# Shorter backlogs for far-ahead transfers, conversions counted in full, and a lighter start, in a conditioned hybrid trunk on eight cores

## The chip, the cores and the metric

The kernel runs on the 8 cores of one Trainium2 chip. Each core handles one batch element with its own copy of the same program; no core talks to another. The metric is the device time of the slowest core, in microseconds (us). In some executions the cores of one die, or of both, show a lower granted TensorE clock and the time is longer, as in one run of the changed kernel: 5797.3 us, with 0.815 on cores 0 to 3 and 0.992 or 0.993 on the others. Such runs are marked and left out. Below, "fast run" means a run without that mark; the fast runs of one kernel in one set lie within 0.3% of each other, except in E7 (0.9%) and E12 (0.6%).

## The reference

Two layers, each with a SwiGLU half step, a mixer and a second SwiGLU half step; shift, scale and gate of every step come from c. Cut to its skeleton:

```python
for l in range(DEPTH):
    mod = silu(c) @ ada_w[l] + ada_b[l]                    # 9 x 1024 values
    y = modulate(rmsnorm(h, norm_g[l, 0]), sh1, sc1)
    h = h + 0.5 * g1 * swiglu(y, ffn1_wg[l], ffn1_wu[l], ffn1_wd[l])
    y = modulate(rmsnorm(h, norm_g[l, 1]), sh2, sc2)
    u, v, q, k, w = split(y @ w_in[l])
    h = h + g2 * (concat(spatial_gating(u, v), dilated_mixture(rope(q), rope(k), w)) @ w_out[l])
    y = modulate(rmsnorm(h, norm_g[l, 2]), sh3, sc3)
    h = h + 0.5 * g3 * swiglu(y, ffn2_wg[l], ffn2_wu[l], ffn2_wd[l])
return rmsnorm(h, final_g)
```

A core has 4096 positions in 8 tiles of 512. The weights arrive as float32 and are turned to bfloat16 once, by transfers from HBM to HBM that convert ("conversions", `wguS<-wgu`, `wdS<-wd`).

## The kernel before

The kernel is a list of thousands of tasks with their dependencies. A scheduler in the program walks through them with a small model of the five engines and of the DMA pipe and writes one fixed instruction order for each engine, with the semaphore waits. On the chip nothing of the model is left but this order. The parts that matter:

```python
def schedule(self, bw=300.0, dlat=2300.0, dmargin=3000.0, cmargin=250.0, backlog=9000.0):
    ...
                if t.dma:
                    if pipe[0] - now > backlog:            # modelled work already in the DMA pipe, ns
                        nxt = min(nxt, pipe[0] - backlog)
                        continue
    ...
            if t.dma:
                pipe[0] = max(pipe[0], st + dur) + t.nbytes / bw
                t.end = pipe[0] + dlat
```

`t.L` is the time by which a task should be done, `hp` the position of the TensorE stream. The start loads c, four constants, tile 0 of x, 16 rows of ada_w (512 KB each), tile 1 of x:

```python
            src = bass.AP(cv.tensor, cv.offset, [[0, 128], [1, D]])          # one row of c to 128 partitions
            G.dma("sp", lambda e: e.dma_start(out=cb, in_=src), 524288, writes=[bcb], name="cb", ...)
    ...
                G.dma("pool", ..., in_=wgu_d[l, w, j]), 1048576, name="guf", ...
                      extra=[first[(10, 12, 14, 15, 19)[min(j, 4)]]] if j < 6 else ())   # first: 16 ada rows, then x tile 1
    ...
            G.chain(ins, [bk], "nsum", pos=pos)            # norm sum of a tile, on TensorE
```

The softmax here doesn't subtract the row's maximum and nothing guards it: scores larger than these inputs give would overflow.

Of the kernel before, what the change touches and what calls it, by code (L numbers as in the profile page):

```python
# [10 lines left out]
ALU = mybir.AluOpType  # L11
# [57 lines left out]
class Graph:  # L69
# [145 lines left out]
    def schedule(self, bw=300.0, dlat=2300.0, dmargin=3000.0, cmargin=250.0, backlog=9000.0):  # L215
# [65 lines left out]
        def pick(e, now):  # L281
# [26 lines left out]
            for t in av:  # L308
# [16 lines left out]
                if t.dma:  # L325
                    if pipe[0] - now > backlog:
                        nxt = min(nxt, pipe[0] - backlog)
                        continue
                    if pipe[0] - now > 3000.0 and any(x.dma and x.eng is None and x.L < t.L and not x.new
                                                      for x in avail["pool" if e == "sp" else "sp"]):  # L330
                        nxt = min(nxt, now + 200.0)
                        continue
# [244 lines left out]
def build_nc():  # L577
# [8 lines left out]
    ada_b = din("ada_b", [128, DEPTH * 72])  # L586
    ngv = din("ngv", [128, DEPTH * 3 * KC])
    fgv = din("fgv", [128, KC])
# [5 lines left out]
    lngb_d = din("lngb", [128, DEPTH * 8])  # L594
# [20 lines left out]
    with ExitStack() as st:  # L615
# [86 lines left out]
        adab = const([128, DEPTH * 72], F32)  # L702
        Av = const([128, DEPTH * 3 * KC], F32)
        Gv = const([128, DEPTH * 3 * KC], F32)
        ng_sb = const([128, DEPTH * 3 * KC], F32)
        fg_sb = const([128, KC], F32)
# [3 lines left out]
        lngb = const([128, DEPTH * 8], F32)  # L710
# [3 lines left out]
        bC = {n: Buf(n) for n in ("ones", "mean", "eps", "ng", "fg", "adab", "lngb", "bc", "ws", "mk")}  # L714
# [18 lines left out]
        sq_more = []  # L733
# [23 lines left out]
        def cond(chunks, pos, slots, cslot, due=None):  # L757
# [4 lines left out]
            tb, btb = tile(slots[0], [128, D], F32, 1, "ct")  # L762
            src = bass.AP(cv.tensor, cv.offset, [[0, 128], [1, D]])
            G.dma("sp", lambda e: e.dma_start(out=cb, in_=src), 524288, writes=[bcb], name="cb", pos=p0,
                  due=None if due is None else due - 150000.0)
            G.op([act(lambda e: e.activation(out=tb, in_=cb, func=AF.Tanh, scale=0.5), 960, "tanh")],
                 reads=[bcb], writes=[btb], name="ctanh", pos=p0)
            G.op([dve(lambda e: e.scalar_tensor_tensor(out=cb, in0=tb, scalar=1.0, in1=cb, op0=ALU.add, op1=ALU.mult), 1150)],
                 reads=[btb], writes=[bcb], name="csilu", pos=p0)
            ring = Ring(slots[1:] + slots[:1], [128, D], F32, "ada")  # L770
            rows = []
            for n, ch in enumerate(chunks):
# [10 lines left out]
                if k in (15, 23):  # L783
# [4 lines left out]
                         reads=[bRow[l][i][part], bC["adab"]], writes=[bm], name="adab", pos=p)  # L788
                    if part == 0:
                        G.op([dve(lambda e, b0=b0, c0=c0: e.scalar_tensor_tensor(  # L790
                            out=Av[:, b0:b0 + KC], in0=modv[:, c0 + 8:c0 + 16], scalar=1.0, in1=ng_sb[:, b0:b0 + KC],
                            op0=ALU.add, op1=ALU.mult), 130)], reads=[bm, bC["ng"]], accw=[bm], name="adaA", pos=p)
# [11 lines left out]
        def load_gu(l, w, j, pos):  # L804
# [3 lines left out]
            if (l, w) == (0, 0) and (l, w, j) not in kept:  # L808
                G.dma("pool", lambda e: e.dma_start(out=ap, in_=wgu_d[l, w, j]), 1048576, writes=[b], name="guf", pos=pos,
                      due={0: -41000.0, 1: -31000.0, 2: -25000.0, 3: -24000.0, 4: -1000.0}.get(j), extra=[first[(10, 12, 14, 15, 19)[min(j, 4)]]] if j < 6 else ())  # L810
# [20 lines left out]
        def conv(l, w, spans, gates=True):  # L831
# [4 lines left out]
            for (j, m), x in zip(items, wt):  # L836
# [8 lines left out]
                if j is not None:  # L845
                    G.dma("pool", lambda e, j=j: e.dma_start(out=wguS[l, w, j], in_=wgu_d[l, w, j]), 1048576,
                          writes=[bWG[l, w, j]], name="cvg", pos=p, extra=[gate])
                else:
                    G.dma("pool", lambda e, m=m: e.dma_start(out=wdS[l, w, m], in_=wd_d[l, w, m]), 1441792,
# [24 lines left out]
        def norm_sum(ht, pos, alts=0):  # L874
# [28 lines left out]
            G.chain(ins, [bk], "nsum", pos=pos)  # L903
# [26 lines left out]
        def norm_out(ht, t, pos, fine=False):  # L930
            rs, brs = norm_sum(ht, pos, 2 if fine else 0)
            for kc in range(KC):
# [4 lines left out]
                     reads=[brs, bC["fg"]], writes=[bh], name="fin", pos=pos)  # L937
# [83 lines left out]
        class Mixer:  # L1021
# [48 lines left out]
            def spatial_tables(self):  # L1070
# [15 lines left out]
                for hd in range(4):  # L1086
# [3 lines left out]
                        reads=[bk, bC["lngb"]], writes=[bC["bc"]], name="bc")  # L1090

            def proj(self, t):
# [104 lines left out]
                def gating(hd, pos):  # L1197
# [9 lines left out]
                        reads=[bk, bC["bc"], bC["lngb"]], writes=[bzt], name="zt", pos=pos)  # L1207
# [244 lines left out]
        for ap, src, n in ((ng_sb, ngv, "ng"), (adab, ada_b, "adab"), (fg_sb, fgv, "fg"), (lngb, lngb_d, "lngb")):  # L1452
            G.dma("sp", lambda e, ap=ap, src=src: e.dma_start(out=ap, in_=src), 65536, writes=[bC[n]], name="const", pos=-20000.0, due=-100000.0)
# [6 lines left out]
        for l in range(DEPTH):  # L1460
# [16 lines left out]
            if l == 0:  # L1477
                for b_ in range(2):
                    for pc_ in range(2):
                        G.dma("pool", lambda e, b_=b_, pc_=pc_: e.dma_start(  # L1480
                            out=mk_sb[:, :, b_ * 256 + pc_ * 128:b_ * 256 + pc_ * 128 + 128],
                            in_=mk_d[:, :, pc_ * 256 + b_ * 128:pc_ * 256 + b_ * 128 + 128]), 196608, accw=[bC["mk"]], name="mk", pos=100000.0,
                              extra=[marks[8][1]])
                conv(0, 0, [(p1 + 40000.0, pg)], False)
                cond(range(16, 48), (p1 + 30000.0, pg - 20000.0), steps(WD0 + 4096, 4096, 3), WD0)
# [128 lines left out]
def _consts():  # L1614
# [11 lines left out]
    for i, (o, k) in enumerate(((pi, n16), (q4, 4 * n16), (n16, n16))):  # L1626
        prev = (k[:, None] >= o[None, :]).astype(np.float32)
        cur = (k[:, None] <= o[None, :]).astype(np.float32)
        masks[:, i] = np.concatenate([prev, prev, cur, cur], 1)
# [19 lines left out]
def _prep_inputs(x, c, ada_w, ada_b, norm_g, ffn1_wg, ffn1_wu, ffn1_wd, ffn2_wg, ffn2_wu, ffn2_wd,  # L1649
# [15 lines left out]
        "ada_b": np.ascontiguousarray(ada_b.reshape(DEPTH, 72, 128).transpose(2, 0, 1).reshape(128, DEPTH * 72)),  # L1665
        "ngv": np.ascontiguousarray(norm_g.reshape(DEPTH, 3, KC, 128).transpose(3, 0, 1, 2).reshape(128, DEPTH * 3 * KC)),
        "fgv": np.ascontiguousarray(f(final_g).reshape(KC, 128).T),
# [4 lines left out]
        "lngb": np.ascontiguousarray(np.concatenate([lng, lnb], 2).reshape(128, DEPTH * 8)),  # L1672
# [19 lines left out]
```

## Time and profile before

| | kernel before |
|---|---|
| fast runs at first | 4884.7 and 4891.1 us |
| spans of the cores | 4860.4 to 4888.1 us |
| TensorE busy, slowest core | 4755.4 us, 97% |
| DMA transfers, share of the chain of waits that ended last | 5% |

TensorE is the bound; what can be won is its idle time, and this lies at the start, around the two mixers and at the end. The lines are in the prediction below. This is SyncE's queue on core 1 where the attention of the first mixer is about to begin (start us, time to hand the transfer over in us, transfer; L1340 below is the first matmul on K):

```profile
684.41 4.87 SPq L825 DMA_DIRECT2D arena<-wdS  x1
689.37 0.51 SPq L1182 DMA_DIRECT2D kS<-arena  x1
689.97 0.97 SPq L1194 DMA_DIRECT2D vS<-arena  x1
691.03 1.26 SPq L1182 DMA_DIRECT2D kS<-arena  x1
...
707.01 0.33 SPq L1271 DMA_DIRECT2D arena<-kS  x1
```

The wdS load at 684.41 us brings down-projection weights, and the next matmul on any such weights comes at 879.45 us. SyncE needs 4.87 us to hand it over (0.33 us for the one at 678.43); that the queue was full is my guess, which no line shows. Only then come the last stores of K. In the chain of waits the K store then takes 15.76 us and the load of K 12.09 us, and TensorE stands still for it (start us, length; idle and what ended it in brackets):

```profile
691.03 15.76 DMA kS<-arena
707.01 12.09 DMA arena<-kS
```

### The profile page before, as it was taken

Reading aid. Unit: us, or ns where it says so; the run is one execution under the profiler, and the core shown is the slowest. Engines: PE = TensorE matmul, PEld = TensorE weight load, DVE = VectorE, ACT = ScalarE, POOL = GpSimd, SP = SyncE. Lnnn points to the kernel's source line nnn. Section 1 sums busy time; section 2 is a strip of 40 time slices with the busy share of each in tenths; the row PEclk is TensorE's granted clock in tenths of the full one; section 3 lists DMA queues with packets and bytes.
Section 4 is the critical chain, followed back from the end, with each engine's and each line's share of the span. In section 5 each row is a group of like instructions: output and inputs, shape, how many; then the busy total and the mean of one; then the engine's idle time right before and its main releaser. Section 6 shows DMA issues by size and latency. Waiting matters only on the chain.

```text
span 4888.1 us, 74266 instructions; the slowest of 8 cores (4860.4 to 4888.1 us)
## 1 busy us (share of the span) xinstructions
PE 4755.4 (97%) x25855; PEld 2250.5 (46%) x25855; DVE 2466.9 (50%) x4087; ACT 2026.2 (41%) x3009; POOL 987.9 (20%) x954
## 2 busy tenths in 40 slices
PE   5999989999999999999999999999999999999998
PEld 2444435454445454444444444454444455544443
DVE  6551556483665473665334326555536554535533
ACT  4111566462755342521311127655537543525311
POOL 0001451112531111300100016312135100122101
PEclk9999999999999999999999999999999999999999
DMA  9987676688475677764721375766665644473414
GB/s 237 200 170 188 169 197 167 180 229 212 157 219 161 186 207 224 213 190 141 243 80 39 92 223 151 209 152 183 154 181 170 193 135 150 118 246 128 142 42 157
DMA packets 376095, 835.32 MB, mean 171 GB/s; under 512 B 151440, under 2 KB 184592, under 8 KB 369296
## 3 DMA queue, kind: packets, MB, share of 16 engines
q1 hardware_dynamic: 356944, 742.08, 49.5%
q0 software_dynamic: 18784, 88.49, 11.8%
q8 instruction: 213, 3.49, 0.3%
q14 instruction: 154, 1.26, 0.1%
HBM read 741.72 MB, written 234.88 MB: 200 GB/s over the span
## 4 chain that ended last, share of the span: by engine, by line
PE 86%; DMA 5%; ACT 3%; DVE 2%; issue 2%; SPq 1%; POOL 1%; DVEq 0%; ACTq 0%; POOLq 0%
PE ps L967 47%; PE ps L995 24%; PE ps L1106 5%; PE ps L1432 4%; PE ps L1374 3%; PE ps L1340 2%; DMA arena<-xP 1%; DMA hS<-arena 1%; DMA arena<-hS 1%; DVE arena L1171 1%; ACT arena L1149 1%; DMA kS<-arena 0%; POOL arena L1147 0%; SPq L778 0%; POOL arena L1178 0%
## 5 line engine op out<-in xcount | busy, mean ns | idle before, releaser
L967 PE MATMUL ps<-arena 128*128 128x512 bf16 x11264 | 2502.9, 380 | 36.2 <-DVE arena L924 28.3
L967 PEld LDWEIGHTS ps<-arena 128*128 128x128 bf16 x11264 | 1082.6, 98 | 1311.9 <-issue 61.2
L995 PE MATMUL ps<-arena 128*128 128x512 bf16 x5632 | 1229.6, 379 | 4.1 <-DVE arena L999 4.1
L973 ACT ACTIVATE arena<-ps 128x512 f32<-128x512 f32 x704 | 418.1, 597 | 1281.3 <-PE ps L967 1277.0
L975 DVE SCALAR_TENSOR_TENSOR arena<-arena,ps 128x512 f32<-128x512 f32 x704 | 480.1, 684 | 765.3 <-ACT arena L973 764.5
L995 PEld LDWEIGHTS ps<-arena 128*128 128x128 bf16 x5632 | 547.1, 98 | 658.2 <-issue 7.5
L999 DVE SCALAR_TENSOR_TENSOR arena<-ps,arena 128x512 f32<-128x512 f32 x256 | 192.0, 750 | 910.1 <-PE ps L995 879.2
L898 POOL TENSOR_TENSOR arena<-arena 128x512 f32<-128x512 f32 (+2 forms) x351 | 414.3, 1180 | 1160.4 <-ACT arena L891 1056.9
L980 DVE TENSOR_TENSOR arena<-ps,arena 128x512 bf16<-128x512 f32 x704 | 483.7, 690 | 211.2 <-PE ps L967 191.3
L1106 PE MATMUL ps<-arena 128*128 128x512 bf16 x2560 | 567.7, 380 | 15.1 <-ACT arena L1190 4.5
L891 ACT ACTIVATE arena<-arena 128x512 bf16<-128x512 f32 x424 | 250.5, 625 | 723.9 <-DVE arena L999 384.6
L1358 ACT ACTIVATE arena<-ps 128x1024 bf16<-128x1024 f32 (+1 forms) x384 | 345.0, 950 | 270.0 <-PE ps L1340 269.1
L1106 PEld LDWEIGHTS ps<-arena 128*128 128x128 bf16 x2560 | 248.7, 98 | 314.3 <-issue 25.2
L1361 DVE TENSOR_TENSOR arena<-arena 128x1024 bf16<-128x1024 bf16 (+1 forms) x384 | 261.5, 687 | 148.7 <-ACT arena L1358 146.4
L926 ACT ACTIVATE arena<-arena 128x512 bf16<-128x512 f32 x372 | 279.5, 806 | 52.3 <-DVE arena L920 51.9
L920 DVE TENSOR_TENSOR arena<-arena 128x512 f32<-128x512 f32 x384 | 271.9, 757 | 35.7 <-ACT arena L906 30.4
L1410 POOL TENSOR_TENSOR arena<-arena 64x512 bf16<-64x512 f32 x128 | 168.4, 1316 | 598.5 <-ACT arena L1405 557.9
L1432 PE MATMUL ps<-arena 128*128 128x512 bf16 x1024 | 225.1, 379 | 2.8 <-DMA arena<-mS 1.8
L1390 DVE TENSOR_TENSOR arena<-ps,arena 128x512 f32<-128x512 f32 x256 | 175.4, 685 | 68.7 <-PE ps L1374 63.1
L1374 PEld LDWEIGHTS ps<-arena 128*128 128x128 bf16 x2736 | 175.4, 98 | 73.8 <-issue 12.9
L1374 PE MATMUL ps<-arena 128*128 128x128 bf16 x2736 | 199.2, 219 | 7.4 <-DVE arena L1361 6.8
L1178 POOL TENSOR_TENSOR arena<-arena 128x512 bf16<-128x512 f32 x128 | 168.4, 1324 | 165.8 <-DVE arena L1169 115.1
(68 smaller groups left out, 2116.0 us busy)
## 6 DMA issues: line engine op xcount, KB each, us to landing
arena<-wguS SPq DMA_DIRECT2D x242, 512.0 KB, 5.6
arena<-hS SPq DMA_DIRECT2D x180, 512.0 KB, 7.9
arena<-wdS SPq DMA_DIRECT2D x128, 704.0 KB, 5.8
arena<-ada_w SPq DMA_DIRECT2D x144, 512.0 KB, 20.1
hS<-arena SPq DMA_DIRECT2D x224, 256.0 KB, 6.2
arena<-hS SPq DMA_DIRECT2D x136, 256.0 KB, 7.8
wguS<-wgu POOLq DMA_DIRECT2D x66, 512.0 KB, 7.8
hS<-arena SPq DMA_DIRECT2D x64, 512.0 KB, 8.2
```

Of the source, the lines that this page charges most:

```text
L898: f = lambda e, a=a, sq=sq, out=out: e.tensor_tensor(out=out, in0=a, in1=sq, op=ALU.add)
L920: f = lambda e, hk=hk, u=u: e.tensor_tensor(out=u, in0=hk, in1=rs, op=ALU.mult)
L926: ga = act(lambda e, hk=hk, A=A, sh=sh, o=o: e.activation(out=o, in_=hk, func=AF.Identity, scale=A, bias=sh), 725)
L967: mate = main([(lambda e, kc=kc, half=half, bk=bk, y=y, gu=gu: e.matmul(bank(bk), lhsT=gu[:, half, kc, :], rhs=y[:, kc, :], start=(kc == 0 ...
L973: G.op([act(lambda e, sg=sg, gb=gb: e.activation(out=smv[sg.i], in_=bank(gb), func=AF.Tanh, scale=0.5), 490, "tanh")], reads=[gb], writes= ...
L975: G.op([dve(lambda e, sg=sg, gb=gb: e.scalar_tensor_tensor(out=smv[sg.i], in0=smv[sg.i], scalar=1.0, in1=bank(gb), op0=ALU.add, op1=ALU.mu ...
L980: G.op([dve(lambda e, sg=sg, ub=ub, o=o: e.tensor_tensor(out=o, in0=bank(ub), in1=smv[sg.i], op=ALU.mult), 610)], reads=[ub, sg], writes=[ ...
L995: main([(lambda e, j=j: e.matmul(bank(bk), lhsT=wd[:, j, :], rhs=a[:, j, :], start=(j == 0), stop=(j == FC - 1)), [bwd, ba[j]], MM) for j ...
L1106: ins.append((lambda e, lhs=lhs, rhs=rhs, kc=kc: e.matmul(bank(bk), lhsT=lhs, rhs=rhs, start=(kc == 0), stop=(kc == KC - 1)), rd + [by[kc] ...
L1358: return e.activation(out=cut(pT, 0), in_=cut(ps[:, :, :], sb.i * 512), func=AF.Exp, scale=0.125)
L1374: return e.matmul(o, lhsT=v[:, vi, h * 64:h * 64 + 128], rhs=pT[:, h, b, pc, :], start=(pc == 0 or not prev), stop=(pc == 1))
L1432: main([(lambda e, kc=kc, m=m, bk=bk: e.matmul(bank(bk), lhsT=w[:, m, kc, :], rhs=mx[:, kc, :], start=(kc == 0), stop=(kc == KC - 1)), [bw ...
```

## The change

The intent: transfers that are needed late should enter the queue only when it is nearly empty; the model should believe in less bandwidth (270 for 300 bytes per ns) and count both the read and the written bytes of a conversion; and the start should load less, in a better order. The diff, cut to its core (the new mask layout and the renamed buffers are left out):

```diff
-    def schedule(self, bw=300.0, ..., backlog=9000.0):
+    def schedule(self, bw=270.0, ..., backlog=9000.0):
-                    if pipe[0] - now > backlog:
-                        nxt = min(nxt, pipe[0] - backlog)
+                    far = t.L - hp
+                    bl = backlog if far < 12000.0 or now < 100000.0 else 5000.0 if far < 40000.0 else 2500.0
+                    if pipe[0] - now > bl:
+                        nxt = min(nxt, max(pipe[0] - bl, now + 50.0) if bl == backlog else now + 200.0)
                         continue
@@ conv
-                    G.dma("pool", ... wgu_d ..., 1048576, name="cvg")   / wd_d ..., 1441792, name="cvd"
+                    G.dma("pool", ... wgu_d ..., 1572864, name="cvg")   / wd_d ..., 2162688, name="cvd"
@@ cond, at the start only
-            G.dma("sp", cb <- c spread to 128 partitions, 524288)
+            G.dma("sp", cr <- c, one row, 4096); tanh and silu on the row
+            for n in range(2): matmul(bank, lhsT=one, rhs=cr[:, n * T:n * T + T]); activation(cb[...] <- bank)
@@ constants
-        four loads: ng_sb, adab, fg_sb, lngb
+        G.dma("sp", lambda e: e.dma_start(out=cst, in_=cst_d), 131072, ..., due=-85000.0)
@@ first gate/up weights
-   extra=[first[(10, 12, 14, 15, 19)[min(j, 4)]]]
+   extra=[first[(10, 12, 17, 19)[min(j, 3)]]]
@@ norm sum of tile 1
+                nsums[1].soft.append(marks[9][1])
+                nsums[1].deps.add(marks[9][1])
@@ masks
-        four loads of 196608
+        one load of 786432
```

I call the first three the ordering edits and the others the start edits; the gate of the weights and the later norm sum together are the tile 1 edits.

More of the change, by code (lines that the diff above doesn't have):

```diff
@@ L213, with schedule @@
     RESERVE = 2
-    def schedule(self, bw=300.0, dlat=2300.0, dmargin=3000.0, cmargin=250.0, backlog=9000.0):
+    def schedule(self, bw=270.0, dlat=2300.0, dmargin=3000.0, cmargin=250.0, backlog=9000.0):
         pend = {e: [] for e in ENG}
@@ L585, in build_nc @@
     ada_w = din("ada_w", [DEPTH * 72, 128, D])
-    ada_b = din("ada_b", [128, DEPTH * 72])
-    ngv = din("ngv", [128, DEPTH * 3 * KC])
-    fgv = din("fgv", [128, KC])
     wgu_d = din("wgu", [DEPTH, 2, FC, 128, 2, KC, 128])
@@ L593, in build_nc @@
     wsT_d = din("wsT", [DEPTH, 128, 4, 128])
-    lngb_d = din("lngb", [128, DEPTH * 8])
+    cst_d = din("cst", [128, DEPTH * 104 + 8])
     bs_d = din("bs_row", [DEPTH, 1, 512])
@@ L701, in build_nc @@
         modv = const([128, DEPTH * 72], F32)
-        adab = const([128, DEPTH * 72], F32)
+        cst = const([128, DEPTH * 104 + 8], F32)
+        adab, ng_sb, lngb, fg_sb = (cst[:, a:b] for a, b in ((0, DEPTH * 72), (DEPTH * 72, DEPTH * 96), (DEPTH * 96, DEPTH * 104),
+                                                             (DEPTH * 104, DEPTH * 104 + 8)))
         Av = const([128, DEPTH * 3 * KC], F32)
         Gv = const([128, DEPTH * 3 * KC], F32)
-        ng_sb = const([128, DEPTH * 3 * KC], F32)
-        fg_sb = const([128, KC], F32)
         ones_bf = const([128, 128], BF16)
@@ L709, in build_nc @@
         eps_sb = const([128, 1], F32)
-        lngb = const([128, DEPTH * 8], F32)
         sgu_bc = const([128, 4, 128], F32)
@@ L713, in build_nc @@
         mk_sb = const([128, 3, 512], BF16)
-        bC = {n: Buf(n) for n in ("ones", "mean", "eps", "ng", "fg", "adab", "lngb", "bc", "ws", "mk")}
+        bC = {n: Buf(n) for n in ("ones", "mean", "eps", "cst", "bc", "ws", "mk")}
         bMod = [[[Buf("mod") for _ in range(2)] for _ in range(3)] for _ in range(DEPTH)]
@@ L732, in build_nc @@
         nuR = Ring(steps(NM, 2048, 2), [128, T], F32, "nu")
-        sq_more = []
+        sq_more, nsums = [], []
         sqE = Ring(steps(ACT[0] + 20480, 1024, 2) + steps(ACT[1] + 16384, 1024, 6), [128, T], BF16, "sq")
@@ L761, in cond @@
             cb, bcb = tile(cslot, [128, D], F32, 1, "cb")
-            tb, btb = tile(slots[0], [128, D], F32, 1, "ct")
-            src = bass.AP(cv.tensor, cv.offset, [[0, 128], [1, D]])
-            G.dma("sp", lambda e: e.dma_start(out=cb, in_=src), 524288, writes=[bcb], name="cb", pos=p0,
-                  due=None if due is None else due - 150000.0)
-            G.op([act(lambda e: e.activation(out=tb, in_=cb, func=AF.Tanh, scale=0.5), 960, "tanh")],
-                 reads=[bcb], writes=[btb], name="ctanh", pos=p0)
@@ L768, in cond @@
-            G.op([dve(lambda e: e.scalar_tensor_tensor(out=cb, in0=tb, scalar=1.0, in1=cb, op0=ALU.add, op1=ALU.mult), 1150)],
-                 reads=[btb], writes=[bcb], name="csilu", pos=p0)
-            ring = Ring(slots[1:] + slots[:1], [128, D], F32, "ada")
+            if due is not None:
+                one, bone = tile(Y0 + 3 * 8192, [1, 128], F32, 1, "one")
+                cr, bcr = tile(Y0 + 3 * 8192 + 512, [1, D], F32, 1, "cr")
+                tr, btr = tile(Y0 + 2 * 8192, [1, D], F32, 1, "tr")
+                memset(one, 1.0, bone)
+                G.dma("sp", lambda e: e.dma_start(out=cr, in_=cv), 4096, writes=[bcr], name="cb", pos=p0, due=due - 150000.0)
+                G.op([act(lambda e: e.activation(out=tr, in_=cr, func=AF.Tanh, scale=0.5), 960, "tanh")],
+                     reads=[bcr], writes=[btr], name="ctanh", pos=p0)
+                G.op([dve(lambda e: e.scalar_tensor_tensor(out=cr, in0=tr, scalar=1.0, in1=cr, op0=ALU.add, op1=ALU.mult), 1150)],
+                     reads=[btr], writes=[bcr], name="csilu", pos=p0)
+                for n in range(2):
+                    bk = Bank()
+                    G.chain([(lambda e, n=n, bk=bk: e.matmul(bank(bk), lhsT=one, rhs=cr[:, n * T:n * T + T], start=True, stop=True),
+                              [bcr, bone], 1800.0)], [bk], "crow", pos=-40000.0)
+                    G.op([act(lambda e, n=n, bk=bk: e.activation(out=cb[:, n * T:n * T + T], in_=bank(bk), func=AF.Identity), 490)],
+                         reads=[bk], accw=[bcb], name="ccopy", pos=p0)
+            else:
+                tb, btb = tile(slots[0], [128, D], F32, 1, "ct")
+                src = bass.AP(cv.tensor, cv.offset, [[0, 128], [1, D]])
+                G.dma("sp", lambda e: e.dma_start(out=cb, in_=src), 524288, writes=[bcb], name="cb", pos=p0)
+                G.op([act(lambda e: e.activation(out=tb, in_=cb, func=AF.Tanh, scale=0.5), 960, "tanh")],
+                     reads=[bcb], writes=[btb], name="ctanh", pos=p0)
+                G.op([dve(lambda e: e.scalar_tensor_tensor(out=cb, in0=tb, scalar=1.0, in1=cb, op0=ALU.add, op1=ALU.mult), 1150)],
+                     reads=[btb], writes=[bcb], name="csilu", pos=p0)
@@ L771, in cond @@
+            ring = Ring(slots, [128, D], F32, "ada")
             rows = []
@@ L787, in cond @@
                                                                       op=ALU.add), 130)],
-                         reads=[bRow[l][i][part], bC["adab"]], writes=[bm], name="adab", pos=p)
+                         reads=[bRow[l][i][part], bC["cst"]], writes=[bm], name="adab", pos=p)
                     if part == 0:
@@ L791, in cond @@
                             out=Av[:, b0:b0 + KC], in0=modv[:, c0 + 8:c0 + 16], scalar=1.0, in1=ng_sb[:, b0:b0 + KC],
-                            op0=ALU.add, op1=ALU.mult), 130)], reads=[bm, bC["ng"]], accw=[bm], name="adaA", pos=p)
+                            op0=ALU.add, op1=ALU.mult), 130)], reads=[bm, bC["cst"]], accw=[bm], name="adaA", pos=p)
                     else:
@@ L809, in load_gu @@
                 G.dma("pool", lambda e: e.dma_start(out=ap, in_=wgu_d[l, w, j]), 1048576, writes=[b], name="guf", pos=pos,
-                      due={0: -41000.0, 1: -31000.0, 2: -25000.0, 3: -24000.0, 4: -1000.0}.get(j), extra=[first[(10, 12, 14, 15, 19)[min(j, 4)]]] if j < 6 else ())
+                      due={0: -41000.0, 1: -31000.0, 2: -25000.0, 3: -24000.0, 4: -1000.0}.get(j), extra=[first[(10, 12, 17, 19)[min(j, 3)]]] if j < 6 else ())
                 G.dma("sp", lambda e: e.dma_start(out=wguS[l, w, j], in_=ap), 524288, reads=[b], writes=[bWG[l, w, j]],
@@ L845, in conv @@
                 if j is not None:
-                    G.dma("pool", lambda e, j=j: e.dma_start(out=wguS[l, w, j], in_=wgu_d[l, w, j]), 1048576,
+                    G.dma("pool", lambda e, j=j: e.dma_start(out=wguS[l, w, j], in_=wgu_d[l, w, j]), 1572864,
                           writes=[bWG[l, w, j]], name="cvg", pos=p, extra=[gate])
                 else:
-                    G.dma("pool", lambda e, m=m: e.dma_start(out=wdS[l, w, m], in_=wd_d[l, w, m]), 1441792,
+                    G.dma("pool", lambda e, m=m: e.dma_start(out=wdS[l, w, m], in_=wd_d[l, w, m]), 2162688,
                           writes=[bWD[l, w, m]], name="cvd", pos=p, extra=[gate])
@@ L902, in norm_sum @@
                 ins = [(lambda e: e.matmul(bank(bk), lhsT=mean_bf, rhs=sb, start=True, stop=True), [bsb, bC["mean"]], MM)]
-            G.chain(ins, [bk], "nsum", pos=pos)
+            nsums.append(G.chain(ins, [bk], "nsum", pos=pos))
             G.op([act(lambda e: e.activation(out=rs, in_=bank(bk), func=AF.Ln, bias=eps_sb), 590, "ln")],
@@ L936, in norm_out @@
                                                                          op1=ALU.mult), 680)],
-                     reads=[brs, bC["fg"]], writes=[bh], name="fin", pos=pos)
+                     reads=[brs, bC["cst"]], writes=[bh], name="fin", pos=pos)
                 if fine or kc % 2:
@@ L1089, in spatial_tables @@
                         scalar=lngb[:, l * 8 + 4 + hd:l * 8 + 5 + hd], in1=sgu_bc[:, hd, :], op0=ALU.mult, op1=ALU.add), 250)],
-                        reads=[bk, bC["lngb"]], writes=[bC["bc"]], name="bc")
+                        reads=[bk, bC["cst"]], writes=[bC["bc"]], name="bc")
             def proj(self, t):
@@ L1206, in gating @@
                         scalar=lngb[:, l * 8 + hd:l * 8 + hd + 1], in1=bcb, op0=ALU.mult, op1=ALU.add), 670)],
-                        reads=[bk, bC["bc"], bC["lngb"]], writes=[bzt], name="zt", pos=pos)
+                        reads=[bk, bC["bc"], bC["cst"]], writes=[bzt], name="zt", pos=pos)
                     f = lambda e: e.tensor_tensor(out=oa[:, hd, :], in0=zt, in1=ugs[hd][0], op=ALU.mult)
@@ L1448, in norm_load @@
             return ht
-        for ap, src, n in ((ng_sb, ngv, "ng"), (adab, ada_b, "adab"), (fg_sb, fgv, "fg"), (lngb, lngb_d, "lngb")):
-            G.dma("sp", lambda e, ap=ap, src=src: e.dma_start(out=ap, in_=src), 65536, writes=[bC[n]], name="const", pos=-20000.0, due=-100000.0)
+        G.dma("sp", lambda e: e.dma_start(out=cst, in_=cst_d), 131072, writes=[bC["cst"]], name="const", pos=-20000.0, due=-85000.0)
         memset(ones_bf, 1.0, bC["ones"])
@@ L1477, in build_nc @@
             if l == 0:
-                for b_ in range(2):
-                    for pc_ in range(2):
-                        G.dma("pool", lambda e, b_=b_, pc_=pc_: e.dma_start(
-                            out=mk_sb[:, :, b_ * 256 + pc_ * 128:b_ * 256 + pc_ * 128 + 128],
-                            in_=mk_d[:, :, pc_ * 256 + b_ * 128:pc_ * 256 + b_ * 128 + 128]), 196608, accw=[bC["mk"]], name="mk", pos=100000.0,
-                              extra=[marks[8][1]])
+                nsums[1].soft.append(marks[9][1])
+                nsums[1].deps.add(marks[9][1])
+                G.dma("pool", lambda e: e.dma_start(out=mk_sb, in_=mk_d), 786432, writes=[bC["mk"]], name="mk", pos=100000.0,
+                      extra=[marks[8][1]])
                 conv(0, 0, [(p1 + 40000.0, pg)], False)
@@ L1628, in _consts @@
         cur = (k[:, None] <= o[None, :]).astype(np.float32)
-        masks[:, i] = np.concatenate([prev, prev, cur, cur], 1)
+        masks[:, i] = np.concatenate([prev, cur, prev, cur], 1)
     return np.ascontiguousarray(rope), tril, masks
@@ L1664, in _prep_inputs @@
         "ada_w": np.ascontiguousarray(ada_w.transpose(0, 2, 1)).reshape(DEPTH * 72, 128, D),
-        "ada_b": np.ascontiguousarray(ada_b.reshape(DEPTH, 72, 128).transpose(2, 0, 1).reshape(128, DEPTH * 72)),
-        "ngv": np.ascontiguousarray(norm_g.reshape(DEPTH, 3, KC, 128).transpose(3, 0, 1, 2).reshape(128, DEPTH * 3 * KC)),
-        "fgv": np.ascontiguousarray(f(final_g).reshape(KC, 128).T),
+        "cst": np.ascontiguousarray(np.concatenate([
+            ada_b.reshape(DEPTH, 72, 128).transpose(2, 0, 1).reshape(128, DEPTH * 72),
+            norm_g.reshape(DEPTH, 3, KC, 128).transpose(3, 0, 1, 2).reshape(128, DEPTH * 3 * KC),
+            np.concatenate([lng, lnb], 2).reshape(128, DEPTH * 8), f(final_g).reshape(KC, 128).T], 1)),
         "wgu": np.ascontiguousarray(wgu), "wd": np.ascontiguousarray(wd),
@@ L1671, in _prep_inputs @@
         "wsT": np.ascontiguousarray(sgu_w[:, :, pi][:, :, :, pi].transpose(0, 3, 1, 2)),
-        "lngb": np.ascontiguousarray(np.concatenate([lng, lnb], 2).reshape(128, DEPTH * 8)),
         "bs_row": np.ascontiguousarray(sgu_b[:, :, pi].reshape(DEPTH, 1, 512)),
```

## The prediction

The 310 and 290 GB/s are my estimates, from the 220 to 368 GB/s that core 1 shows from 10 to 50 us (303 on average); the 2.5 us at which the stream starts and the 3.5 us for the row of c are guesses of mine that no line shows.

> **What bounds the kernel now.** I first read the list of cores, then the busy times, then the table of stretches of the slowest core, then that core's TensorE timeline, and last the DMA rate of the first microseconds.
>
> ```profile
> core 1: 4888.1 us, clock 0.995
> core 3: 4860.4 us, clock 0.997
> ...
> PE 4755.4 (97%) x25855; PEld 2250.5 (46%) x25855; DVE 2466.9 (50%) x4087; ACT 2026.2 (41%) x3009; POOL 987.9 (20%) x954
> ```
>
> No core is throttled, and TensorE is busy for 97% of the span of the slowest core; the next engine has half of that. The chain of waits says the same: 86% of it is matmuls, 5% DMA. In the longest unbroken piece of that chain 1256 matmuls take 271.09 us, 0.2158 us each. None of the edits removes a matmul of the main stream, so all that can be won is time in which TensorE waits. On core 1 that is 4888.1 - 4755.4 = 132.7 us. The table of stretches of core 1 (length, TensorE busy, the other engines, clock, DMA share, GB/s) says where:
>
> ```profile
> 0.00:50.40 50.40, 0.58 (x1) 0.13 (x2) 31.06 (x52) 9.54 (x13) 2.88 (x11) 1.00 0.93 261
> 50.40:66.50 16.10, 9.01 (x24) 2.62 (x25) 4.32 (x9) 6.47 (x10) 1.05 (x2) 0.87 1.01 218
> 66.50:440.00 373.50, 373.50 (x1726) 169.13 (x1725) 182.45 (x287) 90.42 (x143) 29.02 (x46) 1.00 0.82 185
> 440.00:800.00 360.00, 334.30 (x1743) 155.35 (x1742) 193.90 (x379) 203.90 (x323) 147.46 (x138) 0.98 0.74 192
> 2900.00:3250.00 350.00, 335.01 (x1850) 158.17 (x1848) 208.30 (x403) 224.84 (x351) 142.85 (x128) 0.99 0.65 179
> 4800.00:4888.10 88.10, 71.39 (x331) 32.10 (x328) 41.62 (x61) 15.56 (x25) 2.86 (x3) 0.93 0.44 159
> ```
>
> Idle: 49.8 us before the first gate matmul, 7.1 us just after it, none to 440 us, 25.7 us around the first mixer (440 to 800), 15.0 us around the second layer's mixer, 16.7 us in the tail; the two long stretches not shown lose 12.1 and 6.4 us. A change that touches the start and the order of transfers has some 50 + 7 + 26 + 15 us to work on, and most of the 50 is the loading that must precede the first matmul.
>
> The TensorE timeline shows the start (start us, us, operation, count, idle before):
>
> ```profile
> 50.40 6.20 PE L967 MATMUL ps<-arena 128*128 128x512 bf16 x16 [28.29 <-DVE arena L924]
> 56.44 0.59 PE L886 MATMUL ps<-arena 128*128 128x512 bf16 x2
> 57.39 0.90 PE L886 MATMUL ps<-arena 128*128 128x512 bf16 x2 [0.35 <-ACT arena L884]
> 61.20 0.90 PE L886 MATMUL ps<-arena 128*128 128x512 bf16 x2 [2.91 <-ACT arena L884]
> 65.63 1.11 PE L886 MATMUL ps<-arena 128*128 128x512 bf16 x2 [3.54 <-ACT arena L884]
> 66.53 18.77 PE L967 MATMUL ps<-arena 128*128 128x512 bf16 x80
> ```
>
> [...] It does one gate/up pair of tile 0 (16 matmuls), then meets the norm sum of tile 1 (L886, 8 matmuls), which waits for the squares of an x tile that lands in four pieces until 64.8 us (ScalarE's timeline, released by DMA from xP). From 56.6 to 66.5 us, 9.9 us, it does 8 x 0.2158 = 1.7 us of work. All cores show this: gates start at 46.2 to 50.4 us and resume at 61.2 to 66.5 us.
>
> What holds back the first gate is the last of 16 ada_w rows: it lands at 47.6 us (end of VectorE's idle before its row product), and adab, A and y follow in 2.8 us. Up to there the DMA engines are full, but not fast. In 5 us pieces:
>
> ```profile
> 5.00:10.00 5.00, 0.00 (x0) 0.00 (x0) 0.00 (x0) 1.87 (x2) 0.00 (x0) 1.00 0.86 115
> 10.00:15.00 5.00, 0.00 (x0) 0.00 (x0) 1.61 (x2) 2.00 (x4) 0.00 (x0) 1.00 1.01 282
> 15.00:20.00 5.00, 0.00 (x0) 0.00 (x0) 3.37 (x6) 3.06 (x6) 0.00 (x0) 1.00 0.97 368
> ```
>
> Between 5 and 10 us the engines are 86% busy but move 115 GB/s, a third of what they do next. What lies in the queue then is the 512 KB spread of c to 128 partitions (issued at 1.07 us; its tanh starts at 8.12 us) and four constant loads with runs of 32 to 576 bytes.
>
> [...]
>
> **The change part by part.**
> (1) Spread of c. Removed at the start: a 512 KB load. Added: a 4 KB load, two one-row float32 matmuls, two ScalarE copies of 128x512 (0.6 us each like L973); tanh and silu take the same time on one partition (1.06 and 1.23 us). Estimate of when c is ready: row at 3.5, table and tanh 2.4, silu 1.4, two matmuls at the 1.8 us the program books (no such matmul in the trace), copies and hops 1.8: 12.7 us, against 11.8 now. VectorE does not read it before 21 us, so this is hidden. TensorE is idle then.
> (2) Constants: four loads of 108 KB together, at 0.47 us of SyncE issue each, become one with 864-byte runs, placed behind tile 0 of x.
> Both give the DMA stream time. Up to 10 us it moved 5 x 73 + 5 x 115 = 0.94 MB; 0.63 MB of that goes (the rest of the consts is only moved back). The remaining 0.31 MB at 310 GB/s from 2.5 us would be done at 3.5 us, not at 10: 6.5 us at most. Some of the slow start may be just the start, so I take **5 us** for every ada_w row and thus for the first gate: 50.4 to about 45.4 us on core 1.
> (3) Norm sum of tile 1 now comes after the second gate/up pair of tile 0, and the third and later gate/up weights wait for tile 1 of x, not for ada_w rows 14 and 15. Two 1 MB loads leave the way of x, so that x lands 2.1 MB / 290 GB/s = 7 us earlier beside the 5. The lost time was 9.9 - 1.7 = 8.2 us, plus some 6 matmuls at half clock, 1.3 us: 9.5 us. In it now go 16 more matmuls, but weights 2 and 3 come later by the same bytes, and may leave holes of 1 to 4 us. I take **6 us**.
> (4) Bandwidth 270 for 300, 2.5 or 5 us of backlog for transfers needed more than 40 or 12 us later, conversions booked at 1.5 times the bytes. No byte goes. In 440 to 800 us the slowest core is idle 25.7 us, core 3, with the same program, 12.1, core 0 15.0. The chain there holds on core 1 DMA hS<-arena of 16.3 and 18.8 us and arena<-xP of 14.7, which core 3's chain lacks. That 13.6 us is thus contention of transfers, and fewer far-ahead ones in the queue should take about half: **6 us**. In 2900 to 3250 the cores differ by 3.5 us: **1 us**.
> (5) Masks in one load instead of four: 3.0 us of GpSimd issue at 70 us, first needed by attention at about 720: nothing.
> Sum: 5 + 6 + 6 + 1 = 18 us. The reordering also moves ada rows, conversions and reloads behind waits they were ahead of; I take off 1 us. 4889 (the two fast runs have 4884.7 and 4891.1) - 17 = **4872 us**.
>
> **Rivals.** (a) The start is hidden anyway: TensorE starts earlier, runs out of weights 2 and 3, and meets tile 2 of x too soon, since DMA is full until 100 us (share 1.0). For it: that share. Against it: from 66 us TensorE never waits, and 4 tiles of one weight pair are 64 x 0.216 = 13.8 us of work per 1 MB. Then the first 11 us shrink to 4, about 4879. (b) The far-ahead rule costs: weights or h tiles come late because they were held back and then stand behind a SyncE wait; for it, 12.1 us idle in 2100 us (800 to 2900) says that today's early order hides nearly everything. Then 5 to 20 us are added: 4880 to 4890. (c) Contention was the whole loss of the slow cores: all eight come to core 3's time and start 11 us earlier, 4860 - 11 = 4849.
>
> **Range and chances.** (c) gives the low end, (b) with a start that gains little the high end: 4850 to 4892. Faster by 2% would be 98 us; idle time that these edits touch is about that in all, with the loading that can't go: 0.01. Slower by 2% needs a stall repeated in many stages: 0.02. Same: 0.97.
>
> **What would show it.** First gate matmul of core 1 near 45 us; DMA over 250 GB/s from 5 us; 32 gate matmuls before L886's successor and gaps under 4 us there; idle of 440 to 800 us near 20 us on the slowest core, with a smaller spread of cores; no new idle in 800 to 2900. It is wrong if new waits of TensorE on DMA of weights (wguS, wdS, hS) appear in the long stretches, or if c's row path, not ada_w, ends the wait of the first gate.

## More of the kernel before

```profile
719.35 1.04 PE L1340 MATMUL ps<-arena 64*128 64x128 bf16 x12 [8.00 <-DMA arena<-kS]
```

The first two lines are of the chain, the third of TensorE's timeline: 8.00 us are lost at one place, behind a transfer that was needed 190 us later. The lines show the 4.87 us of the hand-over; how much of the 15.76 and 12.09 us other queued transfers cost, they don't show.

## The result, and the profile after

All ratios below are the mean time of one kernel's fast runs over that of the other's fast runs of the same rounds, so they are not quite the ratio of the medians. The interval after a ratio is at 95%.

The changed kernel ran at 4858.0 to 4862.6 us in its five fast runs, against 4884.7 to 4891.1 us in three fast runs of the kernel before: **ratio 0.9946** (0.9928 to 0.9964). That is within 2%, and 4861.8 us lies in the predicted range. But this first number understates the change. The list of cores shows it:

```profile
core 1: 4832.4 us, clock 0.997
core 2: 4859.5 us, clock 0.992
core 3: 4855.5 us, clock 0.992
```

The same program takes 27 us less on core 1 than on core 2. In 5 us pieces of 1215 to 1270 us, core 2 and then core 1 (length, TensorE busy and matmuls, ..., granted clock, DMA share, GB/s):

```profile
1215.00:1220.00 5.00, 5.00 (x21) 2.07 (x19) 1.38 (x2) 3.77 (x10) 0.15 (x1) 0.81 0.27 74
1265.00:1270.00 5.00, 5.00 (x21) 2.08 (x20) 3.58 (x4) 3.62 (x10) 5.00 (x5) 0.81 0.18 54
```

```profile
1215.00:1220.00 5.00, 5.00 (x25) 2.25 (x23) 2.13 (x3) 5.00 (x14) 0.61 (x2) 1.00 0.73 89
1265.00:1270.00 5.00, 5.00 (x25) 2.23 (x24) 2.11 (x3) 4.98 (x14) 5.00 (x6) 1.00 0.37 87
```

TensorE is busy throughout on both, but core 2 does 21 matmuls where core 1 does 25, at a granted clock of 0.81. In the clock records of this trace, 0.81 stands for nine stretches of 15.1 us on cores 2 and 3, for 27 stretches of 3 to 8 us on cores 4 and 5, for 20 on cores 6 and 7, and for one of 15.1 us on cores 0 and 1. That is 136, 147, 100 and 15 us, of which (1 - clock), with the 0.8125 of the records, is lost: 25.5, 27.4, 18.7 and 2.8 us. The traces of the kernel before, of E5 and of E12 have no such record on any core. I take this for a mild form of the slow state, too small for its mark; in the slow run of the same set cores 0 to 3 had 0.815 on average and took 5789 to 5796 us. In two later sets, on chips 11 and 9, the unaltered changed kernel had nearly all its fast runs without it (E5 and E12; 0.997 or 0.998 on all eight cores of the trace of E5): 4836.0 to 4837.8 us, ratio **0.9906** (0.9889 to 0.9922), and 4837.9 to 4840.8 us with one run at 4865.9. In that one, only cores 2 and 3 had a low clock (0.991 and 0.992) and long spans (4860 and 4864 us); all others ended by 4840 us. So the undisturbed effect is about -46 us, where I predicted -17. Whether the changed kernel falls into this state more often than the kernel before stays open: no core of the latter was under 0.993 in a fast run.

For the profile after I therefore use the undisturbed run E5, of another set than the profile before (spans 4828.3 to 4836.2 us; the spread between cores fell from 28 to 8 us). The same stretches of core 1 as in the prediction:

```profile
5.00:10.00 5.00, 3.43 (x4) 1.15 (x4) 1.91 (x2) 1.94 (x4) 0.00 (x0) 1.00 0.99 241
0.00:50.40 50.40, 10.80 (x23) 3.35 (x24) 33.90 (x58) 13.41 (x21) 4.11 (x14) 1.00 0.95 278
50.40:66.50 16.10, 13.80 (x65) 5.94 (x63) 8.10 (x13) 13.69 (x21) 0.18 (x1) 1.00 1.03 224
66.50:440.00 373.50, 370.65 (x1710) 167.47 (x1709) 177.56 (x279) 80.41 (x128) 29.80 (x48) 1.00 0.83 185
440.00:800.00 360.00, 356.57 (x1933) 168.47 (x1932) 210.68 (x409) 228.94 (x356) 152.53 (x144) 1.00 0.78 200
2900.00:3250.00 350.00, 346.20 (x2038) 167.90 (x2036) 223.59 (x430) 229.64 (x356) 140.80 (x130) 1.00 0.72 179
```

From 440 to 800 us the idle time fell from 25.7 to 3.4 us, and 1933 matmuls fit where 1743 did. Core 3, which I had taken as the floor, fell from 12.1 to 2.6 us as well. No DMA piece is left in the chain of waits of core 1 there, where the kernel before had seven of 6.9 to 18.8 us, 98.8 us in all. The place of the K store in SyncE's queue is now this:

```profile
656.41 1.87 SPq L1196 DMA_DIRECT2D kS<-arena  x2
...
668.21 0.33 SPq L1285 DMA_DIRECT2D arena<-kS  x1
...
698.96 0.42 SPq L839 DMA_DIRECT2D arena<-wdS  x1
```

The loads of down weights come after the load of K. From the last K store to the first matmul on K pass 21.8 us, where it was 28.3, and TensorE does not stand still before it. At the start, 2.9 us of new idle appear after 66.5 us. Where core 1's 51.9 us (4888.1 - 4836.2) went, by the start of the same matmul in both traces (counted within its source line):

| up to | before, us | E5, us | won in this part, us |
|---|---|---|---|
| first gate matmul | 50.4 | 43.9 | 6.5 |
| first down matmul | 371.8 | 363.2 | 2.1 |
| first output projection | 1257.3 | 1213.5 | 35.2 |
| 1906th input projection matmul (layer 2's mixer) | 3085.7 | 3039.5 | 2.4 |
| last TensorE instruction's start | 4873.3 | 4821.4 | 5.7 |

The third row needs care, because the new order moved work across its mark: before the first output projection stand 800 input projection matmuls in the kernel before and 768 in E5. These 32 are 6.9 us, so about 28 us of the 35.2 were won there, and about 9 rather than 2.4 in the next part, which holds layer 2's mixer. Core 1 was the worst core of the kernel before. Core 3 went from 869.0 to 851.0 us between the first down matmul and the first output projection, 18 us, of which 11 are won and 6.9 moved in the same way.

### The profile page after: what moved, and what is told of

Read it like the earlier page. It is cut to its first block, busy times and chain, and to the rows that moved or that the text cites. A ratio compares the mean times of both kernels' runs of the same rounds, so it can differ in the third digit from the quotient of the medians.

```text
span 4859.5 us, 74224 instructions; the slowest of 8 cores (4832.4 to 4859.5 us)
## 1 busy us (share of the span) xinstructions
PE 4773.8 (98%) x25859; PEld 2255.6 (46%) x25859; DVE 2459.2 (51%) x4088; ACT 2019.5 (42%) x3005; POOL 977.3 (20%) x951
## 3 DMA queue, kind: packets, MB, share of 16 engines
q0 software_dynamic: 17328, 88.49, 12.7%
## 4 chain that ended last, share of the span: by engine, by line
PE 93%; ACT 2%; DMA 2%; DVE 2%; issue 1%; POOL 1%; SPq 1%; DVEq 0%; ACTq 0%; POOLq 0%
PE ps L981 48%; PE ps L1009 25%; PE ps L1120 10%; PE ps L1446 5%; PE ps L1388 3%; PE ps L1354 2%; DMA arena<-xP 1%; DVE arena L1185 0%; SPq L792 0%; DMA arena<-wguS 0%; DMA arena<-hS 0%; PE ps L1213 0%; DVE arena L949 0%; DMA arena<-wdS 0%; POOL arena L1192 0%
```

## The experiments

**E1, start edits alone.** My theory after the first look was that the ordering edits did the middle and the start edits little; the rival, that an earlier start had freed the middle.

```diff
 (changed kernel)  bw=270.0 -> 300.0; the far rule -> the old test; 1572864 -> 1048576, 2162688 -> 1441792
```

> The changed kernel with the old ordering rules (bandwidth 300, one backlog of 9 us, conversions at their old bytes); c from one row, constants in one load, the later norm sum of tile 1, the new gate of weights 2 and 3 and the one mask load stay. Theory: the start is worth about 4 us (the first down matmul at 363 to 367 us instead of 367 to 372) and the idle of 440 to 800 us stays at 12 to 26 us, so about 4884 us, slowest core 4875 to 4886, and no stretches of granted clock 0.81. Rival: the middle was freed by the earlier start, so that this run too idles under 6 us in 440 to 800 and ends near 4862.

Measured: 4901.9 to 4907.7 us in three fast runs, ratio 1.0032 (1.0003 to 1.0061). The rival falls, and so does my theory of a gain of 4 us: the start edits alone cost time. Core 3 shows how (TensorE's timeline):

```profile
44.57 9.33 PE L979 MATMUL ps<-arena 128*128 128x512 bf16 x32 [28.09 <-DVE arena L936]
...
78.17 1.89 PE L979 MATMUL ps<-arena 128*128 128x512 bf16 x8
84.94 4.96 PE L979 MATMUL ps<-arena 128*128 128x512 bf16 x8 [4.88 <-ACT arena L938]
89.70 2.06 PE L898 MATMUL ps<-arena 128*128 128x512 bf16 x8
```

The first gate comes 3.1 us earlier (mean of the cores 44.3 for 47.4 us) and now 32 matmuls run before the norm sum of tile 1, as meant. Then TensorE waits 4.88 us for the y of a later tile and takes 4.96 us for the next 8 matmuls, at a granted clock of 0.50 and while y comes in piece by piece (six of their weight loads are 0.70 us apart). The first down matmul comes at 374.9 us (mean of the cores) instead of 368.9: the wait had only moved, and grown by 6 us. The idle of the middle stayed (13.9, 21.5, 24.9 and 24.1 us on cores 0, 1, 3 and 5).

**E2 and E6, ordering edits alone**, on two chips.

```diff
 (kernel before)  bw=300.0 -> 270.0; + far rule; 1048576 -> 1572864, 1441792 -> 2162688
```

> The kernel before with the three ordering edits alone (bandwidth 270, short backlog for far transfers, conversions at 1.5 times the bytes). Theory: idle in 440 to 800 us falls from 12 to 26 to under 8 us and in 2900 to 3250 from 12 to 17 to under 6; start as before (first gate at 46 to 50 us); cores that keep the clock end at 4838 to 4845, about 4866 by the slowest core if clock 0.81 stretches come back as in the changed kernel, 4845 if they do not. Rival (the start edits did it): 4885 and the old idle.

> The kernel before with the three ordering edits alone, once more, beside the changed kernel. If the 0.81 stretches belong to the chip, this one shows them too when the changed kernel does and the two end within 5 us of each other; if the start edits bring them on, this one keeps 0.997 on all cores and 4837 to 4839 us, about 22 us under the changed kernel.

Measured: 4837.0 to 4839.1 us, ratio 0.9899 (0.9856 to 0.9941), and 4836.1 to 4837.9 us, ratio 0.9906 (0.9886 to 0.9926). Idle of 440 to 800 us: 2.3 to 5.4 us on the eight cores of E6. In the second set it ran beside the changed kernel (E5), and both have the same ratio. The three ordering edits are the whole gain. The question of E6, whether the start edits bring on the 0.81 stretches, it could not answer, since the changed kernel beside it had none. In no fast run of the two did a core's mean clock fall under 0.996.

**E3, the far rule alone.**

```diff
 (kernel before)  + far = t.L - hp ; bl = 9000, 5000 or 2500 ns
```

> The kernel before with the far-ahead rule alone. Theory that this rule is the main one of the three: at least two thirds of what the three ordering edits win together, so 4860 to 4872, idle of 440 to 800 us under 10. Rival (the booked bandwidth and the conversions' bytes do it): 4880 or more, idle of 440 to 800 over 10 us.

Measured: 4863.1 and 4864.8 us, ratio 0.9950 (0.9907 to 0.9992): half of the gain, not two thirds. Idle of 440 to 800 us 4.7 to 12.8 us.

**E8, E9 and E10, booked bandwidth and conversions.**

```diff
 E8 (kernel before)   bw=300.0 -> 270.0; 1048576 -> 1572864, 1441792 -> 2162688
 E9 (kernel before)   1048576 -> 1572864, 1441792 -> 2162688
 E10 (kernel before)  bw=300.0 -> 270.0
```

> The kernel before with bandwidth 270 and the conversions' bytes, without the far-ahead rule. The far rule alone gave 4863 to 4865 and all three 4837 to 4839. Theory that the far rule and these two add: 4858 to 4868 us, with idle of 440 to 800 us at 6 to 15. Rival that they only work together: 4880 or more. Rival that these two do all of it: 4836 to 4842.

> The kernel before with only the conversions booked at 1.5 times their bytes. Bandwidth 270 and conversions together won about 23 us of 4883. Theory: the conversions are spread over 500 to 1200 us where the first mixer idles, and they are most of it: 4862 to 4870. Rival: the booked bandwidth is most of it; then this run stays within 6 us of the kernel before (4877 to 4890).

> The kernel before with only the booked bandwidth changed from 300 to 270. Theory of the start: with 270 the program itself places 32 gate matmuls, not 16, ahead of the norm sum of tile 1, so that the 160th gate matmul comes 2 to 4 us earlier than in the kernel before even without the start edits. Total: if the parts add, this is what remains of 23 us after the conversions' part.

Measured: E8 4858.8 to 4860.7 us, ratio 0.9953 (0.9936 to 0.9969), some 23 us, as its theory had it: with the 25 us of the far rule (E3) this is about what all three win. E9 had one fast run, 4875.2 us, against 4884.2 to 4887.6 of the kernel before: some 11 us. E10 had two, 4856.5 and 4857.6 us: some 29 us. So E9 lies between its two expectations, the bandwidth is the larger of the two parts, and they do not add: 29 and 11 alone give 23 together (from two sets on two chips, with one fast run of E9 and two of E10, so only roughly). E10 also confirms its theory of the start: with 270 the scheduler expects tile 1 of x later and by itself puts 32 gate matmuls ahead of its norm sum,

```profile
45.73 9.02 PE L967 MATMUL ps<-arena 128*128 128x512 bf16 x32 [27.82 <-DVE arena L924]
54.59 1.03 PE L886 MATMUL ps<-arena 128*128 128x512 bf16 x4
```

and the first down matmul comes at 363.8 us (mean of the cores), 5 us earlier than before. That is what the tile 1 edits were to bring by hand.

**E11 and E14, is "far" needed, or only "shorter"?** Both cut the backlog for every transfer to 5 us.

```diff
 E11 (kernel before)  backlog=9000.0 -> 5000.0
 E14 (kernel before)  the same; bw=300.0 -> 270.0; 1048576 -> 1572864, 1441792 -> 2162688
```

> The kernel before with the backlog cut from 9 to 5 us for every transfer, near or far. The far rule alone won about 25 us. Theory that what counts is to hold back the far transfers only: cutting all of them starves the start and the near loads too and wins less than half of that, 4876 or more. Rival, a shorter queue is all that matters: 4858 to 4868, as with the far rule.

> Bandwidth 270, conversions at 1.5 times the bytes, and the backlog cut to 5 us for every transfer in place of the far rule. Theory that what matters is how much is queued in all, not which transfers are held back: 4835 to 4845, as with the far rule. Rival that the distinction matters: 4850 or more, with TensorE waiting in 440 to 800 us for over 8 us on the slowest core or in the first 100 us for late near loads.

Measured: E11 4858.3 to 4866.6 us, ratio 0.9953 (0.9930 to 0.9975), as good as the far rule alone; my theory for E11 was wrong. E14 4860.6 to 4861.7 us, ratio 0.9941 (0.9922 to 0.9960): its theory was wrong too. The other two edits add nothing that stands clear of the intervals, while the far rule with them reaches 0.9899 to 0.9910. So a flat 5 us wins the first half as well as the far rule, and does not win the second. That this is due to the distinction between near and far is likely but not shown alone: the far rule also leaves the first 100 us at 9 us of backlog and goes down to 2.5 us for the farthest transfers, and no run has a flat 2.5 us or a flat 5 us from 100 us on. The idle of E14 in 440 to 800 us is 3.8 to 7.4 us, not over 8 as its rival had it. Part of where it stays behind is shown by who waited for whom on core 2 (us in total, times, longest):

```profile
PE ps L1374 <- DVE arena L1361: 9.9, 11, 2.6
PE ps L995 <- DMA arena<-wdS: 9.1, 2, 4.6
```

Cores 1 and 5 have 8.1 and 8.5 us in the second line, against 1.2 and 1.8 us in E6. So the flat limit seems to hold back weights that are needed soon; that is some 7 of the 23 us by which core 1's spans differ, and the rest is not traced.

**E4, zeros for w_in**, to see whether the stretches of clock 0.81 depend on the operands. The cause that the expectation supposed is cut from it; no run shows one.

```diff
-        "w_in": _colchunks(w_in[:, :, wcols]),
+        "w_in": np.zeros_like(_colchunks(w_in[:, :, wcols])),
```

> The changed kernel with zeros as w_in (result wrong on purpose): the same instructions, but the mixer's projections multiply by zero and q, k, v are zero. Theory that the 0.81 stretches of the mixer stages [...] go away on all cores, every core has a mean clock of 0.995 to 0.998, and the slowest core ends at 4830 to 4840 instead of 4858 to 4861. Rival: the clock is cut by time or by place whatever the operands are; then two or three pairs of cores keep 0.992 and the run ends near 4860.

Measured: one fast run, 4839.0 us, all cores at 0.996 to 0.999. It decides nothing: the changed kernel with live data did the same on other chips (E5, E12), and four of its five runs were slow in spite of the zeros.

**E5 and E12, the changed kernel again**, unaltered.

> The changed kernel once more, unaltered, on the same chip as the three runs sent with it. If the 0.81 stretches belong to the changed program (its start, or the denser middle), two or three pairs of cores again show a clock of 0.991 to 0.994 and the slowest core ends at 4858 to 4863. If they belong to the chip or the moment of the first runs, every core has 0.996 to 0.998 and the slowest core ends at 4835 to 4845.

> The changed kernel a third time, beside its version with the old gating of tile 1. The first runs of it had two or three pairs of cores at 0.991 to 0.994 and ended at 4858 to 4863, the second job at 4836 to 4838 with 0.997 everywhere. If the slower form belongs to one chip or moment: 4835 to 4840 here in its fast runs, ratio 0.989 to 0.991. If the program is on the edge of it: some of the fast runs again at 4855 to 4865, with pairs of cores under 0.995.

Measured, as told above: 0.9906 (0.9889 to 0.9922) and 0.9910 (0.9887 to 0.9934). The stretches do not belong to every run of the program, and lowered clocks in fast runs are on two chips besides the first set (9 in E12, 11 in E7 below); what starts them stays open.

**E7 and E13, the changed kernel with the old handling of tile 1.**

```diff
 (changed kernel)
-                nsums[1].soft.append(marks[9][1])
-                nsums[1].deps.add(marks[9][1])
-   extra=[first[(10, 12, 17, 19)[min(j, 3)]]]
+   extra=[first[(10, 12, 14, 15, 19)[min(j, 4)]]]
```

> The changed kernel with the norm sum of tile 1 and the gates of weights 2 and 3 as before; ordering edits, row of c, one constant load and one mask load stay. Theory that these two gating edits are worth nothing on top of the ordering edits (first down matmul at 363 to 366 us with and without them): within 4 us of the changed kernel at equal clock. Rival (they are the useful part of the start): the first down matmul 4 us or more later, about 4845 us at full clock.

> The changed kernel with the norm sum of tile 1 and the gates of weights 2 and 3 as before. Theory that these two edits cost what the row of c wins: the 160th gate matmul comes 3 to 4 us earlier than in the changed kernel, cores at full clock end 3 us earlier, and the fast runs are at 4831 to 4836, ahead of both kernels. Rival: the lead is lost again by 440 us and both end within 1 us.

Measured: E7 had two fast runs, 4833.3 us, and 4878.7 us with one die at 0.987 to 0.993 (ratio 0.9945, 0.9888 to 1.0002). E13: 4835.1 to 4842.4 us, ratio 0.9893 (0.9879 to 0.9907), beside E12's 4837.9 to 4840.8 without its one disturbed run. The first down matmul comes at 363.6 us in E13 and 365.4 in E12, 362.9 in E5 and 363.2 in E6 (means of the cores). The lead of 3 to 4 us that E13 expected at the 160th gate matmul is nearly there (92.9 us against 95.9 in E12, means of the cores), 1.8 us of it are left at the first down matmul, and nothing in the times, as its rival had it. I don't call this version faster; it shows that the tile 1 edits bring nothing on top of the ordering edits. The same holds for all the start edits, by E5 against E6.

**What no run separates.** The scheduler orders all engines with one model, so each of the three ordering edits changes more than SyncE's queue. Compared matmul by matmul on core 1, TensorE's order first differs from the kernel before at the 1875th matmul in E3, the 2607th in E9 and the 18th in E10 (E2 and E6, the same program on two chips, agree in all 25 855). How much of the gain comes from the transfers' order and how much from work that was moved into waits, as the 32 gate matmuls of E10, is not known.

## Why the prediction was right or wrong

The frame was right: TensorE is the bound, only its idle time can be won, and 2% is out of reach. Even undisturbed, and with all three ordering edits, the gain is 0.9 to 1.0%. The size was wrong: -17 us predicted, about -46 us without the disturbed clock, and the number first measured lies within the range only because the disturbance gave some 25 us back on the slowest cores. That is luck. By its own steps:

- **(1) and (2), c and constants, 5 us for the first gate.** The DMA rate of core 1 from 5 to 10 us rose from 115 to 241 GB/s, just short of the 250 I had named. But the 115 was core 1's own: the other seven cores had 164 to 269 in the same trace. The means of the cores are 192 before, 206 in E6 without these edits, and 260 in E5 (238 to 286 in the first trace of the changed kernel). The first gate came 3.7 us earlier as a mean of the cores (47.4 to 43.8), 6.5 on core 1; E6, without these edits, has 45.8, so they brought some 2 us. The two float32 matmuls became four instructions that took 3.74 us together, 1.87 us a matmul where I had booked 1.8, and were hidden, as said. In the first trace of the changed kernel, on core 1, the row of c was there at 2.57 us, tanh and silu took 1.05 and 1.21 us on one partition, and the second copy ended at 11.6 us, for the 12.7 I had estimated. But nothing of this is left at the first down matmul (362.9 against 363.2 us in E6). Rival (a) happened: the next tile of x and the next weights are not there earlier, and TensorE waits there instead (core 1 of E5: 0.99 and 1.31 us for weights, 2.71 us at a norm sum).
- **(3), tile 1, 6 us.** It fell. The step was that time lost at the norm sum would be filled by 16 more matmuls. It was, but with the old order the wait came back one tile later (+6 us, E1), and with the new one the scheduler had already filled it (E10). The half clock in my sum is in the trace before: core 1 had a granted clock of 0.50 from 66.5 to 69.1 us, and there six weight loads came 0.43 us apart, later 0.22. In the undisturbed trace the start wins 6.0 us (368.9 to 362.9), all of it by the ordering edits, which I had not credited with any at the start.
- **(4), ordering, 7 us: this step failed; the term was mis-sized.** I took core 3's idle of 12.1 us as the floor and half of the difference between cores as the gain. But core 3 suffered from the same queue. I had written that its chain lacks such waits; in fact it lacks only hS and has five DMA pieces of its own from 440 to 800 us (xP 13.2, 12.9 and 16.7, qS 7.3, kS 12.0), 62.0 us in all. After the edits none is left, and its idle, too, fell to 2.6 us. I had also argued that the backlog rule can act in one way only, by where a transfer stands between SyncE's waits. That was not shown, and it was too narrow, as the changed order of TensorE shows. On core 1 about 28 us were won between the first down matmul and the first output projection, where 6 were predicted: of the 35.2 us in the table, 21.2 are idle time (28.0 to 6.8), 6.8 are clock (13.7 us at half clock before, none in E5), and 6.9 are the 32 moved matmuls. In 440 to 800 us the mean clock of core 1 went from 0.98, with 25.7 us of idle, to 1.00, with 3.4. In 2900 to 3250 us the idle of core 1 fell from 15.0 to 3.8 us, 11.2 where I had put 1. The mechanism, far transfers ahead of urgent ones in SyncE's queue, is there in the lines of the K store before (wdS at 684.41 us, the last K store at 691.03) and gone in those after (wdS at 698.96, the last K stores at 656.41); that it is the whole of the gain is not shown, since the order of the engines changed too.
- **(5), masks,** as said: no run shows an effect, and none singles it out.
- **Rival (b)** shows nowhere on core 1: 800 to 2900 us idle 12.1 us before and 11.6 in E5 on core 1. **Rival (c)** comes nearest to the truth with 4849, but is 12 us short for the same reason as step (4).
- **Missing** was any term for a disturbed clock. No step could have foreseen it from the profile before, which has no record of clock 0.81.
- **A small slip:** the longest unbroken piece of the chain is 1408 matmuls in 303.89 us, not 1256; the time of one is 0.2158 us in both.

## What to carry to other kernels

Room to spare on average in the DMA engines did not keep the bound engine from waiting here: they were 74% busy from 440 to 800 us, and TensorE still stood idle for 8.00 us at one place, for a load of K, while a transfer needed 190 us later stood in front of the stores that the load needed. In E5, with the three ordering edits, that wait was gone. Here it paid to hold back the far ones, to keep the near ones free, and to book less bandwidth. When all cores run the same program, the best core is not a floor (core 3 fell from 12.1 to 2.6 us of idle): ask what it waits for, too. And don't read a rate or a wait off the worst core alone: look at all of them. And check the granted clock of every core before taking a small difference for the effect of a change.
